# Row means on one core: two early stores divided by partitions into five DMAs

## The chip, the core and the metric

The kernel runs on one core of a Trainium2 chip. A core has engines that run side by side, each with its own instruction queue: VectorE (DVE in the profile), ScalarE (ACT), GpSimd (POOL), SyncE (SP) and TensorE (PE, unused here). Data move between the device's main memory and the core's on-chip memory of 128 partitions by DMA. An engine's queue issues a DMA, and 16 DMA engines carry out its packets in the background. When its part is through, each DMA engine adds to a semaphore, a counter on which an instruction of any engine can wait. The metric is device time in microseconds (us); lower is better. Before the change it is 160.59 us, the median of three runs (160.5 to 160.63).

## What is computed

The reference divides the sum of each row by a constant, 1024:

```python
batch, seq, dim = 32, 512, 1024
"x": np.random.randn(batch, seq, dim).astype(np.float32)
return (np.sum(x, axis=-1) / divisor).astype(np.float32)
```

That is 16,384 rows of 1,024 floats in (67.1 MB) and 16,384 floats out (0.07 MB).

## The kernel before

**Tiling.** The 16,384 rows are 128 per partition. They stand in two regions. In the first region partition p holds the 15 rows from 15p on; in the second it holds 113 rows, of which the first 97 are the "main" part and the last 16 the "last" part. So there are three outputs: `o_first` (15 floats per partition, 60 bytes), `o_main` (97 floats, 388 bytes, at a step of 113 floats) and `o_last` (16 floats, 64 bytes, in the gaps that `o_main` leaves). The results are gathered on chip in `res0`, `res` and `fin`; the profile calls both of the first two `res`.

**Loads and sums.** Every load is issued by SP through `load` (L182), in program order. They bring 2 and 13 rows per partition (first), then 14, 14, 14, 14, 14, 14 and 13 (main), then 9, 4 and 2 rows (last), and at the end one row in two halves, `pa` and `pb`. The large tiles rotate over three buffers, so a load waits until DVE is done with the tile that had its buffer. DVE reduces the rows of a tile with one instruction (L205); of the last two main tiles ACT takes 4 and 5 rows (L186). POOL multiplies a finished part by 1/1024 (L207). In the last part DVE sums single rows with the scale applied (L192), and ACT shares them. The row that comes in halves is summed last: first `pa` into a spare column of `pb`, then `pb` with that column into `fin`.

**Stores.** SP issues `o_first` (L223) and `o_main` (L224) after the load of `pb`, and `o_last` (L228) at the very end. One queue holds all of SP's DMAs; `tc.keep_in_program_order` fixes their order.

**Semaphores.** The framework gives the DMAs eight semaphores in turn. The seventeen DMAs are fourteen loads and three stores, so `o_first` has the seventh semaphore, `o_main` the eighth and `o_last` the first. Before a DMA is issued, SP waits until the DMA that used its semaphore before has landed, and a store also waits for the instruction that made its data.

**The end, written out by hand.** Three passes run over the finished program. `start_loads_at_once` (L19) moves the loads that wait for nothing ahead of the start barrier. `latest_wait_first` (L50) sorts an instruction's waits. `close_while_storing` (L69) moves the issue of `o_last` into the end sequence: SP first drains its other waits, joins the end barrier, then issues `o_last` when the semaphore `landed` says that DVE's last sum is there. Meanwhile POOL waits for all other DMAs and engines, clears the semaphores and releases the engines. SP's last instruction waits for `o_last` alone:

```python
last = nc.sync.wait_ge(landed, 17).ins
```

POOL's waits come from one list, which stands in the order POOL, ACT, DVE and then the DMA semaphores one to eight, and is compiled into five instructions with two waits each, in the order fourth and third, fifth and second, sixth and first, seventh and DVE, eighth and ACT, and one more for POOL itself.

Of the kernel before, what the change touches and what calls it, by code (L numbers as in the profile page):

```python
# [125 lines left out]
@with_exitstack  # L126
def kernel(
    ctx: ExitStack,
    tc: tile.TileContext,
    x: bass.AP,  # L130
    divisor: float,
    out: bass.AP,
):
    nc = tc.nc
    landed = nc.alloc_semaphore("landed")
    nc.at_finalize(start_loads_at_once)
    nc.at_finalize(latest_wait_first)
    nc.at_finalize(lambda nc: close_while_storing(nc, landed))
    xf = x.flatten_outer_dims()
    N, D = xf.shape  # L140
    P = nc.NUM_PARTITIONS
    scale = 1.0 / float(divisor)
    J = N // P
    assert J * P == N


    F, L = 15, 16
    M = J - F - L
    W = M + L
    x_first = bass.AP(tensor=x.tensor, offset=0, ap=[[F * D, P], [D, F], [1, D]])  # L150
    x_main = bass.AP(tensor=x.tensor, offset=P * F * D, ap=[[W * D, P], [D, M], [1, D]])
    x_last = bass.AP(tensor=x.tensor, offset=P * F * D + M * D, ap=[[W * D, P], [D, L], [1, D]])
    o_first = bass.AP(tensor=out.tensor, offset=0, ap=[[F, P], [1, F]])
    o_main = bass.AP(tensor=out.tensor, offset=P * F, ap=[[W, P], [1, M]])
    o_last = bass.AP(tensor=out.tensor, offset=P * F + M, ap=[[W, P], [1, L]])


    first = [(2, 0), (13, 0)]
    main = [(14, 0)] * 5 + [(14, 4), (13, 5)]
    last = [(9, 4), (4, 2), (2, 1)]  # L160
    assert sum(n for n, _ in first) == F
    assert sum(n for n, _ in main) == M and sum(n for n, _ in last) == L - 1

    pad = ctx.enter_context(tc.tile_pool(name="pad", bufs=1))
    pad.tile([P, 224], F32, name="pad")
    bulk = ctx.enter_context(tc.tile_pool(name="bulk", bufs=3))
    one = ctx.enter_context(tc.tile_pool(name="one", bufs=1))
    psum = ctx.enter_context(tc.tile_pool(name="junk", bufs=4, space=bass.MemoryType.PSUM))


    c = 512
    t4 = one.tile([P, 4, D], F32, name="t4")
    t2 = one.tile([P, 2, D], F32, name="t2")
    pa = one.tile([P, 768], F32, name="pa")[:, :c]
    pb = one.tile([P, D - c + 16], F32, name="pb")[:, : D - c + 2]
    res0 = one.tile([P, F], F32, name="res0")
    res = one.tile([P, M], F32, name="res")
    fin = one.tile([P, L], F32, name="fin")
    nc.gpsimd.memset(pb[:, D - c :], 0.0)  # L179

    def load(dst, src):
        tc.keep_in_program_order(nc.sync.dma_start(out=dst, in_=src))  # L182

    def act_sum(dst, src, by=1.0):
        junk = psum.tile([P, D], F32, name="junk")
        nc.scalar.activation(junk, src, COPY, scale=by, accum_out=dst)  # L186

    def dve_mean(dst, src, by=scale):


        h = src.shape[-1] // 2
        nc.vector.tensor_tensor_reduce(  # L192
            out=src[:, :h], in0=src[:, :h], in1=src[:, h:], scale=by, scalar=0.0,
            op0=ADD, op1=ADD, accum_out=dst,
        )

    for loads, src, dst in ((first, x_first, res0), (main, x_main, res)):
        j = 0
        for rows, on_act in loads:
            t = bulk.tile([P, 14, D], F32, name="t")  # L200
            load(t[:, :rows, :], src[:, j : j + rows, :])
            d = rows - on_act
            for i in range(d, rows):
                act_sum(dst[:, j + i : j + i + 1], t[:, i, :])
            nc.vector.reduce_sum(out=dst[:, j : j + d], in_=t[:, :d, :], axis=AX)  # L205
            j += rows
        nc.gpsimd.tensor_scalar_mul(out=dst, in0=dst, scalar1=scale)  # L207
    j = 0
    for rows, on_act in last:
        t = bulk.tile([P, 14, D], F32, name="t")[:, :rows, :] if rows > 4 else t4 if rows == 4 else t2  # L210
        load(t, x_last[:, j : j + rows, :])
        d = rows - on_act
        for i in range(rows):
            if i < d:
                dve_mean(fin[:, j + i : j + i + 1], t[:, i, :])
            else:
                act_sum(fin[:, j + i : j + i + 1], t[:, i, :], by=scale)
        j += rows
    load(pa, x_last[:, j, :c])
    load(pb[:, : D - c], x_last[:, j, c:])  # L220


    tc.keep_in_program_order(nc.sync.dma_start(out=o_first, in_=res0))  # L223
    tc.keep_in_program_order(nc.sync.dma_start(out=o_main, in_=res))  # L224

    dve_mean(pb[:, D - c : D - c + 1], pa, by=1.0)
    dve_mean(fin[:, j:], pb)
    tc.keep_in_program_order(nc.sync.dma_start(out=o_last, in_=fin))  # L228
# [35 lines left out]
```

## Time and profile before

| | |
|---|---|
| median of 3 runs | 160.59 us |
| span of the profiled execution | 159.1 us |
| profiled execution, to the last record of the runtime's semaphore | 160.53 us |
| DVE busy | 117.2 us (74% of the span) |
| ACT busy | 18.5 us (12%) |
| POOL busy | 1.0 us (1%) |
| DMA queue, share of 16 engines | 98.2% |
| memory traffic over the span | 422 GB/s |

The span runs from the first to the last instruction of the profiled execution; the times of the runs also hold what the runtime does around it, so they are some 1.5 us longer. An engine's busy time is the sum over its instructions; issuing DMAs and waiting for semaphores don't count as busy. A DMA's time to landing runs from the start of its issue to the last of its completion records and includes the time that it stands in the queue. Besides the views that are shown, the trace holds the start of every DMA packet with its size, and the time of every addition to a semaphore; where the text speaks of packet records, completion records or instruction records, it means these.

### The profile page before, as it was taken

How to read it: one execution, taken by the hardware profiler on the slowest of the kernel's cores; microseconds unless marked ns; L12 is line 12 of the kernel's file. 1: busy time of each engine (PE TensorE's matmuls, PEld its weight loads, DVE VectorE, ACT ScalarE, POOL GpSimd, SP SyncE). 2: the span in 40 equal slices, each digit the busy share in tenths (PEclk: the TensorE clock that was granted, in tenths of full speed). 3: DMA queues.
4: the chain of work that ended last, by engine and by line, in shares of the span. 5: the costliest groups of instructions: out<-in, count | busy, mean ns of one | idle time of the engine just before them, and what ended most of it. 6: DMA issues, size and time to landing. Idle time of an engine off the chain costs nothing.

```text
span 159.1 us, 148 instructions
## 1 busy us (share of the span) xinstructions
DVE 117.2 (74%) x29; ACT 18.5 (12%) x33; POOL 1.0 (1%) x7
## 2 busy tenths in 40 slices
DVE  0500089966999599959996899969995993398643
ACT  3000000000000000000000000000003700390684
POOL 0000000000000000000000000000000000001000
DMA  8999979999999789999998799999998999899894
GB/s 329 431 455 455 467 332 433 461 461 461 461 461 447 317 389 461 461 461 461 461 461 346 346 461 461 461 461 461 461 418 351 442 469 442 350 445 445 383 404 153
DMA packets 2448, 67.18 MB, mean 422 GB/s; under 512 B 656, under 2 KB 656, under 8 KB 912
## 3 DMA queue, kind: packets, MB, share of 16 engines
q1 hardware_dynamic: 2448, 67.18, 98.2%
HBM read 67.11 MB, written 0.07 MB: 422 GB/s over the span
## 4 chain that ended last, share of the span: by engine, by line
DMA 77%; DVE 21%; SPq 1%; issue 0%; DVEq 0%
DMA t<-in_x_dram 55%; DMA pb<-in_x_dram 22%; DVE res L205 20%; SPq L182 1%; DVE pb L192 0%; DVEq L259 0%
## 5 line engine op out<-in xcount | busy, mean ns | idle before, releaser
L205 DVE TENSOR_REDUCE res<-t 128x14 f32<-128x14336 f32 (+4 forms) x9 | 111.2, 12360 | 35.1 <-DMA t<-in_x_dram 35.1
L186 ACT ACTIVATE junk<-t 128x1024 f32<-128x1024 f32 x16 | 16.2, 1013 | 136.9 <-DMA t<-in_x_dram 136.9
L192 DVE CUSTOM_DVE_ANT_0 t<-t 128x512 f32<-128x512 f32 x8 | 5.1, 688 | 5.1 <-DMA t<-in_x_dram 5.1
L186 ACT ACTIVATION_READ_ACCUMULATOR junk<-t 128x1 f32 x16 | 3.0, 186 | 0.0
L207 POOL TENSOR_SCALAR res<-res 128x15 f32<-128x15 f32 (+1 forms) x2 | 0.7, 365 | 144.4 <-DVE res L205 144.4
L186 ACT ACT_TABLE_LOAD x1 | 1.3, 1283 | 1.7 <-PEq L245 1.7
L192 DVE DVE_READ_ACCUMULATOR2_ANT fin<- 128x1 f32 x9 | 0.7, 82 | 0.0
L192 DVE CUSTOM_DVE_ANT_0 pb<-pb 128x257 f32<-128x257 f32 x1 | 0.4, 429 | 0.2 <-DMA pb<-in_x_dram 0.2
L192 DVE CUSTOM_DVE_ANT_0 pa<-pa 128x256 f32<-128x256 f32 x1 | 0.4, 426 | 0.0
L179 POOL MEMSET pb<- 128x2 f32 x1 | 0.1, 100 | 1.3 <-POOLq L245 1.3
L245 POOL MEMSET const-bfloat16-1.0<- 128x1 bf16 x1 | 0.1, 102 | 0.0
L245 POOL MEMSET const-uint8-127<- 128x1 uint8 x1 | 0.1, 102 | 0.0
L245 POOL MEMSET const-float32-0.0<- 128x1 f32 x1 | 0.1, 100 | 0.2 <-issue 0.2
L245 POOL MEMSET const-float32-1.0<- 128x1 f32 x1 | 0.1, 99 | 0.0
L192 DVE DVE_READ_ACCUMULATOR2_ANT pb<- 128x1 f32 x1 | 0.1, 84 | 0.0
## 6 DMA issues: line engine op xcount, KB each, us to landing
t<-in_x_dram SPq DMA_DIRECT2D x6, 7168.0 KB, 36.0
t<-in_x_dram SPq DMA_DIRECT2D x2, 6656.0 KB, 27.2
t<-in_x_dram SPq DMA_DIRECT2D x1, 4608.0 KB, 28.4
t<-in_x_dram SPq DMA_DIRECT2D x2, 1024.0 KB, 19.8
t<-in_x_dram SPq DMA_DIRECT2D x1, 2048.0 KB, 32.9
pa<-in_x_dram SPq DMA_DIRECT2D x1, 256.0 KB, 35.1
pb<-in_x_dram SPq DMA_DIRECT2D x1, 256.0 KB, 35.2
out_dram<-res SPq DMA_DIRECT2D x1, 48.5 KB, 10.8
```

The source lines that it names most:

```text
L179: nc.gpsimd.memset(pb[:, D - c :], 0.0)
L182: tc.keep_in_program_order(nc.sync.dma_start(out=dst, in_=src))
L186: nc.scalar.activation(junk, src, COPY, scale=by, accum_out=dst)
L192: nc.vector.tensor_tensor_reduce(out=src[:, :h], in0=src[:, :h], in1=src[:, h:], scale=by, scalar=0.0, op0=ADD, op1=ADD, accum_out=dst,)
L205: nc.vector.reduce_sum(out=dst[:, j : j + d], in_=t[:, :d, :], axis=AX)
L207: nc.gpsimd.tensor_scalar_mul(out=dst, in0=dst, scalar1=scale)
L245: nc = _bacc.Bacc("TRN2", target_bir_lowering=False, num_devices=1)
```

## The change

The two early stores are cut by partitions. `o_first` becomes two DMAs, of partitions 0 to 119 and 120 to 127. `o_main` becomes three, of partitions 0 to 3, 4 to 115 and 116 to 127. All five are issued by SP after the load of `pb`, in this order, and each waits as a store did before: for POOL's scaled result and for the DMA that used its semaphore before. What is stored, and from and to where, stays. The program then has twenty DMAs in place of seventeen; `o_last` takes the fourth semaphore.

```diff
-    tc.keep_in_program_order(nc.sync.dma_start(out=o_first, in_=res0))
-    tc.keep_in_program_order(nc.sync.dma_start(out=o_main, in_=res))
+    def store(dst, src, *cuts):
+        for p0, p1 in zip((0, *cuts), (*cuts, P)):
+            tc.keep_in_program_order(nc.sync.dma_start(out=dst[p0:p1, :], in_=src[p0:p1, :]))
+
+    store(o_first, res0, 120)
+    store(o_main, res, 4, 116)
```

## The prediction

> **What bounds the kernel now.** I read the chain that ended last first, because it says which wait sets the end.
>
> ```profile
> DMA 77%; DVE 21%; SPq 1%; issue 0%; DVEq 0%
> DMA t<-in_x_dram 55%; DMA pb<-in_x_dram 22%; DVE res L205 20%; SPq L182 1%; DVE pb L192 0%; DVEq L259 0%
> ```
>
> No store is on it. In order of time its tail is the last load, one vector operation, and the end sequence:
>
> ```profile
> 121.91 35.22 DMA pb<-in_x_dram
> 157.12 0.02 issue
> 157.15 0.43 DVE pb L192
> 157.57 0.01 DVEq L259
> ```
>
> Next the DMA issues, columns KB and us from issue to landing, and then the SP queue's instructions in time:
>
> ```profile
> pb<-in_x_dram SPq DMA_DIRECT2D x1, 256.0 KB, 35.2
> out_dram<-res SPq DMA_DIRECT2D x1, 48.5 KB, 10.8
> out_dram<-res SPq DMA_DIRECT2D x1, 7.5 KB, 34.9
> out_dram<-fin SPq DMA_DIRECT2D x1, 8.0 KB, 1.4
> ```
> ```profile
> 122.39 0.48 SPq L223 DMA_DIRECT2D out_dram<-res  x1
> 146.95 0.34 SPq L224 DMA_DIRECT2D out_dram<-res  x1
> 157.61 0.33 SPq L228 DMA_DIRECT2D out_dram<-fin  x1
> ```
>
> The early stores are issued long before the end, but they queue behind pb: the first lands at 122.39 + 34.9 = 157.3, the second at 146.95 + 10.8 = 157.8, both after pb at 157.12. The last store goes out at 157.61 and lands at about 159.0. So the end is pb, then 0.45 of DVE, then 1.4 of the last store. What the DMA engines do there, by windows (the last two columns are DMA share and GB/s):
>
> ```profile
> 156.00:157.00 1.00, 0.98 (x4) 1.00 (x2) 0.00 (x0) 1.00 0.84 266
> 157.00:158.00 1.00, 0.43 (x2) 0.05 (x1) 0.00 (x0) 1.00 0.00 1
> 158.00:159.10 1.10, 0.00 (x0) 0.00 (x0) 0.00 (x0) 1.00 0.08 8
> ```
>
> The engines are empty for nearly all of 157 to 158; in the trace's packet records the early stores' last packet is at 157.05 and the last store's first at 158.44. Last, what SP waits for, and the end sequence by its lines:
>
> ```profile
> SPq L224 <- POOL res L207: 24.0, 1, 24.0
> SPq L259 <- ACT junk L186: 9.7, 1, 9.7
> SPq L105 <- SPq L105: 0.5, 1, 0.5
> ```
> ```profile
> L259 POOLq EVENT_SEMAPHORE  x9: 17/42/43, 155.9 to 158.5; - x9
> L105 SPq EVENT_SEMAPHORE  x1: 17/17/17, 159.0 to 159.0; - x1
> ```
>
> SP has 24.0 and 9.7 us of idle time around the second store. The 0.5 before L105 is the slack that matters: POOL, which collects every other completion, is through and has released SP by 158.57, and SP then waits for the last store until 159.05.
>
> **The sum's base.** The page gives the profiled execution a span of 159.1 (159.06 in the trace) and no total. Its records of the runtime's semaphore go on to 160.53, so that is its own time as far as the trace shows it, 0.06 under the median of 160.59. I carry differences to the median.
>
> **The change, part by part.** (1) Three more DMA issues on SP. The two kinds of row are 0.48 and 0.34, so 1.0 to 1.4 us of issue. One is added at about 122.9 inside the 24.0 wait, two at about 147.3 inside the 9.7 wait. Cost 0; if that cover were gone it would be the 1.4. Behind them on SP stands only the last store.
>
> (2) New waits on SP. The eight DMA semaphores are used in turn, and an issue first waits for the earlier DMA on its semaphore. Counting on from the loads: the 8-row piece waits for the sixth 14-row load (landed by 121.93), the 4-row piece for the 13-row load of the main part (137.69), the 112-row piece for the 9-row load (148.54), the 12-row piece for the 4-row load (153.40), the last store for the 2-row load (155.90); the times are the starts of the instructions that waited for these loads in the timeline. So the 112-row piece is issued at about 148.6, the 12-row piece at 153.4 to 153.8, not at 147. Both are still in the queue before pb's packets are through (156.3 to 156.8, 0.44 us between the first and the last engine). The last store's new wait is over 1.7 us before 157.61. Cost 0. The nearest row for how late an issue may be is the last store itself, 0.83 from issue to first packet: 153.8 + 0.8 = 154.6, 1.7 us of cover.
>
> (3) Packets. The bytes and the 256 row packets stay; completion packets grow with the pieces. In the packet records a 60 B packet takes 7 ns of its engine, a 388 B packet 20, a completion 9. If each piece spreads evenly, an engine that gets every remainder has one 60 B, one 388 B and three completions more: 7 + 20 + 27 = 54 ns; an engine left out of the remainders has less than before. All of it is behind pb and ahead of 158.44: 157.05 + 0.05 = 157.10. Cost 0, cover 1.3 us. The other end: one piece falls on a single engine, 112 x 20 ns = 2.24 us, and that engine is busy until about 159.0. I take even spreading, as each of the 17 DMAs here has 16 completion records, one per engine.
>
> (4) Landing of the early stores. The last packet to landing is 0.73 for the second store on its slowest four engines (157.05 to 157.78; the other twelve are in by 157.47), 0.39 for the last store, 0.30 for pb. The last piece therefore lands between 156.97 + 0.30 = 157.3 and 157.10 + 0.73 = 157.8; doubling the worst row gives 158.5. I take 157.7, by the row of the same kind.
>
> (5) POOL's end sequence. Before, POOL's instruction records show five two-semaphore waits: the 2-row and 4-row loads at 155.91, pa at 156.55, pb at 157.15, the first store at 157.32, the second at 157.80, the one that came last, and 0.77 later SP is released. The order goes by semaphore, not by time. After, the 12-row piece sits on the 4-row load's semaphore, thus in the first of the five, and the other four follow only then. The nearest row is 0.09 from that last wait to the instruction behind it, so 4 x 0.09 = 0.35 more. Release then at 157.7 + 0.02 + 0.77 + 0.35 = 158.84, against the last store's 159.05: still 0.2 earlier. Cost 0 to 0.1, I take 0.
>
> Sum: 0 on every part; pb, DVE and the last store untouched. 160.59 + 0.0 = 160.6.
>
> **A rule against it.** The row is the last store's 1.4 us from issue to landing, with SP idle around the early ones. The Trainium skill (DMA: Bandwidth & Descriptors, Rules for kernel authors) says transfers over separate parts of the partitions only serialize and should be one transfer, and its section on the anatomy of one DMA (for the GpSimd path) gives a fixed cost of about 2.0 us each; three more, if each were paid in turn, would be 6 us, 166.6 by an estimate from that page. The trace already shows pa and pb, each 35 us from issue to landing, overlapping.
>
> **The rivals.** (a) Slower by the collection on POOL. For it: step 5's wait order, with only 0.48 us of slack, and other engines that pass the runtime's end may need their release earlier still than SP. Against: the slack is larger than 0.35. It decides when the last piece lands after 157.90; over 0.2% needs 158.2. At 158.5 POOL releases at 159.64 rather than 159.05, 0.6 later: 161.2. At the limit where the slack outside SP's wait is nearer 0.2 than 0.48 and the landing stays 157.78, 0.15 later: 160.75.
>
> (b) Slower by a piece on too few engines. The 112-row piece on one engine ends at about 159.0 or after; that engine's part of the last store then starts at 159.0 in place of 158.5, 0.5 to 0.7 later: 161.1 to 161.3. It decides from about 80 rows on one engine. Against: no DMA here ran on fewer than 16, though none here has a row count other than 128.
>
> (c) Faster, because the last load or the last store no longer shares the slow engines with the early stores. For it: pb's engines end 0.44 apart, and if the stores of the early ones held back the late ones, up to 0.44 would come back, 160.15; the last store's landing of 0.39 could come down to pb's 0.30, 160.5. Against: the first load of the kernel, with no store in the queue, has the same spread (4.25 to 4.70). What lies behind the span, 1.5 us, is not explained by any row and could move either way.
>
> **How the numbers follow.** A measurement of this kernel can tell about 0.2%, 0.32 us, from no change. The main case, everything covered: 0.58, all within, its own range 160.35 to 160.85. Rival (a): 0.16, of it 0.14 slower and 0.02 within. Rival (b): 0.07, slower. Rival (c), with the unexplained end: 0.19, of it 0.17 faster and 0.02 within. So faster 0.17, same 0.62, slower 0.21. The range reaches to 160.15 for most of (c) and to 161.1 for most of (a) and the near end of (b).
>
> **What would show it.** Right: pb still lands at about 157.1 and the last store goes out some 0.5 later and takes 1.4; five early stores with issues near 122.4, 122.9, 147, 148.6 and 153.4, SP idle behind each; SP's last wait at L105 still over 0.1. Step 2 is wrong if the 112- and 12-row issues follow the 4-row one at once; step 3, if DMA share in 157 to 158 is no longer about 0; step 4, if a piece lands after 157.9; step 5, if POOL's five waits end together rather than one after the other. The forecast fails if SP's wait at L105 goes to 0 and the span grows (a), if the last store takes 1.9 or more (b), or if pb's landing moves (c).

## The result and the profile after

The changed kernel takes 161.05 us (median of 4 runs, 160.76 to 161.21) against 160.60 for the kernel before (4 runs beside it). The ratio is 1.0029, with a 95% interval of 1.0017 to 1.0042: 0.29% slower, 0.45 us. The profiled execution of the changed kernel is the slowest of its four, 161.21, with a span of 159.46. The kernel before has a span of 159.06, and its records put its profiled execution at about 160.42 (the last runtime record, less the 0.12 by which this record lies past the run's time in the other profiles). So the two profiled executions differ by 0.8, more than the medians do. The changed kernel was timed twice more in the experiments, at 161.24 and 161.26 against 160.53 and 160.64 for before beside it, 0.71 and 0.62 us slower.

The path that the chain shows has hardly moved. The tail of the chain in order of time, changed kernel (start, us, what):

```profile
122.05 35.12 DMA pb<-in_x_dram
157.16 0.02 issue
157.19 0.43 DVE pb L192
157.62 0.01 DVEq L263
```

pb lands at 157.16 in place of 157.12, and DVE's last sum is as long as before. The stores, in the view of SP's instructions and of the DMA issues (KB, then us to landing; for three of the pieces the view gives no landing):

```profile
122.53 31.20 SPq L225 DMA_DIRECT2D out_dram<-res  x5
157.65 0.36 SPq L232 DMA_DIRECT2D out_dram<-fin  x1
```
```profile
out_dram<-res SPq DMA_DIRECT2D x1, 42.4 KB, 9.5
out_dram<-res SPq DMA_DIRECT2D x1, 7.0 KB, 35.2
out_dram<-res SPq DMA_DIRECT2D x1, 0.5 KB
out_dram<-res SPq DMA_DIRECT2D x1, 1.5 KB
out_dram<-res SPq DMA_DIRECT2D x1, 4.5 KB
out_dram<-fin SPq DMA_DIRECT2D x1, 8.0 KB, 1.4
```

The five early stores are issued between 122.53 and 153.73, the last store goes out at 157.65 (before: 157.61) and still takes 1.4. The DMA engines stay empty after pb, by the window from 157 to 158 (the last two columns are DMA share and GB/s):

```profile
157.00:158.00 1.00, 0.44 (x3) 0.10 (x1) 0.00 (x0) 1.00 0.01 1
```

What moved is the end sequence. Its instructions by line (durations in ns, least, median and greatest; then the first and the last start) and SP's last wait:

```profile
L263 POOLq EVENT_SEMAPHORE  x9: 17/43/2347, 155.9 to 159.3; - x9
L263 SPq EVENT_SEMAPHORE  x3: 17/17/17, 155.9 to 159.4; - x3
L105 SPq EVENT_SEMAPHORE  x1: 17/17/17, 159.4 to 159.4; - x1
```

The last of SP's three is the one that POOL releases. The kernel before had it here:

```profile
L259 SPq EVENT_SEMAPHORE  x3: 17/17/17, 147.3 to 158.6; - x3
```

Before, POOL's nine semaphore instructions took at most 43 ns each and the last began at 158.5. Now one of them is held for 2.35 us and the last begins at 159.3, 0.8 later. SP's last wait begins at 159.4 although the last store has landed at 159.09, and the 0.5 of waiting before L105 is gone from the list of SP's waits. POOL's collection now ends after every other wait.

The instruction and completion records say how. The first of POOL's five two-semaphore waits holds the 12-row piece, whose last completion comes at 158.27. The four waits behind it follow at 0.087 each, and SP is released at 159.36. In the kernel before the last early completion is at 157.78 and the release at 158.57. The 0.80 between the releases is 0.49 of later landing and 0.31 of waits that stand behind the late one (four waits are 0.35; the step right after the late landing is 0.04 shorter than before).

### The profile page after: what moved, and what is told of

It reads as the page before. It is cut to its first block, busy times and chain, and to the rows that moved or that the text cites. A ratio compares the mean times of both kernels' runs of the same rounds, so it can differ in the third digit from the quotient of the medians.

```text
span 159.5 us, 151 instructions
## 1 busy us (share of the span) xinstructions
DVE 117.2 (73%) x29; ACT 18.5 (12%) x33; POOL 1.0 (1%) x7
## 4 chain that ended last, share of the span: by engine, by line
DMA 77%; DVE 21%; SPq 1%; issue 0%; DVEq 0%
DMA t<-in_x_dram 55%; DMA pb<-in_x_dram 22%; DVE res L205 20%; SPq L182 1%; DVE pb L192 0%; DVEq L263 0%
```

## The experiments

**The theory (A in the expectations).** POOL's release sets the time. It comes late for two reasons: more completions on a DMA engine land later, and the last piece's semaphore is first in POOL's order of waits. The rivals: the order costs nothing; pieces on fewer than 16 engines delay the landing by their shape rather than their number; or the added DMAs cost time in the queue itself, whoever waits for them.

**1. The order of POOL's waits turned (e1, and the same kernel again as e11, beside the changed kernel, e12).** The change stays, but the waits for the three pieces of `o_main` and the 8-row piece stand in the last two of the five instructions. The list of waits is put in a new order (`DMAHW0` is the first semaphore; `...` marks what is left out):

```diff
+ORDER = ('Pool_', 'DMAHW1_', 'DMAHW7_', 'DVE_', 'DMAHW5_', 'DMAHW3_', 'DMAHW4_', 'Activation_', 'DMAHW6_', 'DMAHW0_', 'DMAHW2_')
...
-            with_sync(i, on_wait=tuple(needs.values())) if i.name == gather.name else i
+            with_sync(i, on_wait=in_order(needs)) if i.name == gather.name else i
```

In the trace POOL's instructions then wait for fourth and fifth, ACT and sixth, seventh and DVE, first and eighth, second and third.

> The five pieces as changed; only the order of POOL's five end waits is other: the three o_main pieces and the 8-row piece stand in the last two. Theory A (two terms: the last piece lands 0.5 later because each further completion on a DMA engine takes about 0.2, and POOL's wait order adds 0.35 behind it): landing stays near 158.27, release 0.35 earlier, at about 159.05, level with the last store's landing; span 159.1 to 159.2, time 160.6 to 160.8. Theory B (the landing alone decides, the order costs nothing): no change, 161.05. Theory C (the loss is outside POOL's sequence): no change, and SP's last wait stays at 0.1.

Measured: 161.06 (5 runs; ratio to before 1.0034, 1.0022 to 1.0047), no better than the first timing of the changed kernel, but that one was made in another session with other runs of before. In the profile the release did come earlier, at 159.11, as theory A said, with the last landing at 158.32. So I ran it again with the changed kernel on one chip.

> The changed kernel with POOL's waits in the other order (the same kernel as e1), beside the changed kernel on one chip. Order worth 0.3: 0.25 to 0.35 below the changed kernel, 160.85 to 161.0. Order worth nothing, as e1 beside the first timing of the changed kernel looked: level.

> The changed kernel as it is, for the comparison with the reordered waits on this chip: 161.0 to 161.3.

Measured: 160.94 (11 runs; ratio 1.0017, 1.0008 to 1.0026) for the turned order against 161.26 (6 runs; ratio 1.0037, 1.0025 to 1.0049) for the changed kernel, a difference of 0.32. That is what POOL's records say of the order: from the last early landing to the release it is 1.10 us in the changed kernel and 0.79 in e1, 0.31 less. The first pair did not show it, and kernels timed apart can't be compared to better than some 0.2: against the before beside it, the turned order was slower by 0.50 in e1 and 0.30 in e11, the changed kernel by 0.45, 0.71 and 0.62. The second profile of the turned order (e11) shows one more thing: there pb itself landed late on a single DMA engine, at 157.76, and the last store with it.

**2. The order alone, in the kernel before (e4).** Nothing is cut; only the two early stores' semaphores are put into the first of POOL's waits.

```diff
+ORDER = ('Pool_', 'Activation_', 'DVE_', 'DMAHW0_', 'DMAHW1_', 'DMAHW6_', 'DMAHW7_', 'DMAHW4_', 'DMAHW5_', 'DMAHW2_', 'DMAHW3_')
```

POOL then waits for eighth and seventh, fifth and second, sixth and first, third and DVE, fourth and ACT.

> The kernel before, with only the order of POOL's end waits changed: the two early stores' semaphores are waited for first, four waits follow. It measures the order by itself. Theory A: landing 157.78 as before, release 0.35 later at 158.92, still ahead of the last store at 159.05: span 159.1, time 160.6 if SP's slack is the only one, up to 160.8 if the other engines need their release earlier than SP.

Measured: 161.05 (5 runs, 160.81 to 161.47; ratio 1.0033, 1.002 to 1.0045). It is 0.49 slower than before, about as much as the change in its first timing, with no store cut. In the profiled execution (161.47, the slowest) the end sequence reads:

```profile
L266 POOLq EVENT_SEMAPHORE  x9: 17/43/43, 158.5 to 159.6; - x9
L266 SPq EVENT_SEMAPHORE  x3: 17/17/17, 147.5 to 159.6; - x3
```

POOL's first wait is met only at 158.5, because ten completions of the second store came at 158.19 to 158.48 that time. So two things moved the release in this execution, 0.70 of later landing and 0.35 of order, and the order's own share is better read from e11 and e12. The execution still refutes the prediction's slack. The release came 1.05 later than in the kernel before (159.62 for 158.57), and the time rose by 1.05 as well (161.47 for about 160.42), while the end of SP's last instruction moved by only 0.65. Had the time gone by SP's end, as the prediction had it, it would have risen by 0.65.

**3. Each cut alone (e2, then e3).**

```diff
-    store(o_main, res, 4, 116)
+    store(o_main, res)
```

> Only o_first is cut (120 and 8); o_main whole. Theory A: three completions on up to eight engines in place of two, landing 157.78 + 0.2 = 157.98; o_main's semaphore is in POOL's third wait, two waits follow, + 0.17; release 158.95, still under 159.05: span 159.1, time 160.6 to 160.7. If pieces on fewer than 16 engines by themselves delay the landing (theory B2), the landing is near 158.27 and the span 159.3.

Measured: 160.91 (11 runs; ratio 1.0021, 1.0012 to 1.0031), more than expected. The landing is 158.14 and two waits stand behind it (0.14).

```diff
-    store(o_first, res0, 120)
+    store(o_first, res0)
```

> Only o_main is cut (4, 112, 12); o_first whole. Theory A: four completions on the engines with every remainder, landing 157.78 + 2 x 0.2 = 158.1 to 158.2; the 12-row piece is in POOL's second wait, three follow, + 0.26; release 159.15 to 159.25, 0.1 to 0.2 over the last store: span 159.2 to 159.3, time 160.75 to 160.95. If the cut of o_first carries the loss, 160.6.

Measured: 160.81 (11 runs; ratio 1.0018, 1.001 to 1.0027), as expected in time, with a landing of 157.94, earlier than expected, and 0.22 of waits behind it. Neither cut carries the loss alone. They are 0.35 and 0.25 over before; the sum, 0.60, is level with the change itself (0.45, 0.71 and 0.62 in its three timings). The two landings don't go by the count of completions: the DMA engines that had most had three with the first cut (158.14) and four with the second (157.94). With one profile of each, a count can't be told from the spread here; the next two experiments can.

**4. Five even pieces (e5, beside the changed kernel, e8).** As many DMAs as in the change, but each of a multiple of 16 partitions, so that each has 16 completions.

```diff
-    store(o_first, res0, 120)
-    store(o_main, res, 4, 116)
+    store(o_first, res0, 112)
+    store(o_main, res, 16, 112)
```

> Five early stores again, but cut so that each has a multiple of 16 partitions (112 and 16; 16, 96 and 16), so every piece has 16 completions, one per engine. Revised theory A (POOL's second release sets the end: time = last early landing + what POOL's remaining waits cost + 2.64, the sum that the runs so far share to 0.01): what counts is the number of completions on an engine, and that is five on all of them: landing 158.2 to 158.5, time 161.05 to 161.4. Theory B (pieces on 8, 4 or 12 engines delay the landing by their shape): landing back at 157.8 to 158.0, time 160.75 to 160.95.

> The changed kernel as it is, on the same chip as the other three, for their comparison and for the spread of its landing: 160.8 to 161.2, last early landing 158.0 to 158.4.

Measured beside each other: 161.25 (5 runs; ratio 1.0046, 1.0033 to 1.0058) and 161.24 for the changed kernel itself (5 runs; ratio 1.004, 1.0027 to 1.0054). The shape is not it. The landings of the even pieces show the cost plainly. The last completion of pb and of each store after it, in the order of the queue:

```
pb 157.35   stores 157.53  157.71  157.87  158.05  158.25
```

The steps are 0.17 to 0.20. Each further completion behind the last load took this long, though its packet is recorded at 9 ns, and of a piece of 16 partitions an engine has one data packet of at most 24 ns. The fourth piece has 96 partitions, six data packets to an engine, and its step is no longer than the others. The records don't name the engine of a completion; that the steps are those of one engine is read from all 16 records moving alike.

**5. Six even stores (e10).**

```diff
-    store(o_first, res0, 120)
-    store(o_main, res, 4, 116)
+    store(o_first, res0)
+    store(o_main, res, 16, 32, 48, 112)
```

> o_first whole, o_main in five pieces of 16, 16, 16, 64 and 16 partitions: six completions on every engine. If each completion behind the last load takes its engine about 0.18 (the step between the early stores' first and last landings in the even-cut kernel), the last piece lands 6 x 0.18 = 1.1 after pb at 157.2 to 157.3, at 158.3 to 158.5, and with POOL's four waits behind it the time is 161.3 to 161.5, some 0.1 to 0.2 over the five even pieces. If a random delay of single engines decides and not the count, no more than the five: 160.9 to 161.25.

Measured: 161.55 (5 runs; ratio 1.0054, 1.0042 to 1.0066), 0.3 over the five pieces, which ran on another chip (0.2 when each is taken against the before beside it), and 0.3 over the changed kernel on the same chip (161.26). The completion records, first and last of each store:

```
       pb      stores
first  156.79  156.97  157.14  157.32  157.49  157.66  157.84
last   157.28  157.69  157.89  158.10  158.29  158.49  158.70
```

The first completions step by 0.17 and the last by 0.20. The last ones also carry a delay of 0.41 rather than 0.2 at the first store. So the count sets the steps, and on top of them some engines are late by some tenths, in one execution more than in another.

**6. SP waits for the early stores instead of POOL (e6 and e7, then e9).** The stores' completions go to a semaphore that POOL doesn't collect, and SP waits for it at its very end, beside the last store's. First the changed kernel, then the kernel before.

```diff
+    stored = nc.sync.wait_ge(early, 80).ins      # 32 in the kernel before
...
+        else with_sync(i, on_update=on_early("sem-add-imm", 16)) if i.name in firsts
...
+        with_sync(stored, on_update=on_early("sem-sub-imm", 80)),
         with_sync(last, on_update=update("sem-sub-imm", 17)),
```

> The changed kernel, but the five stores' completions go to a semaphore of their own for which SP waits at its very end, beside the last store's; POOL no longer waits for any store. Revised theory A: POOL's waits end with pb and with DVE's part of the barrier at 157.65, its second release comes at 158.3 rather than 159.36, and the whole loss goes: 160.1 to 160.5, at or below the kernel before; how far below says where SP's wait for the last store begins to bind. Rival (the loss lies in the queue or in DGE work of the added DMAs, not in POOL's wait for them): it stays near 161.0.

> The kernel before, with the same move of its two early stores' completions from POOL to SP. Revised theory A: POOL's wait for the second store set the end here too, so it gains: 160.1 to 160.5, the same as the changed kernel with that move. Rival (before was bound by SP's wait for the last store, as the prediction read L105): 160.56, no change.

Measured: 160.78 (11 runs; ratio 1.0013, 1.0004 to 1.0022) and 160.51 (11 runs; ratio 0.9997, 0.9988 to 1.0006). The first is above the 160.1 to 160.5 that theory A expected. The changed kernel ran at 161.24 on that chip, so most of the loss goes with POOL's wait. The kernel before gains nothing from the same move, against theory A too: it was not bound by POOL alone. What is left of the loss, 0.25, came with a late pb (157.49 in the profile). So I gave each of the five stores a semaphore of its own:

> As e6 (the changed kernel, SP instead of POOL waits for the five early stores), but each store has a semaphore of its own. e6 was left 0.25 above before, with pb's last two engines 0.3 behind the others. If the 80 additions to one semaphore caused that: 160.5, level with e7. If the five DMAs behind pb cost it themselves (through pb's landing and the longer issue of the last store, 0.36 for 0.33): 160.75 again.

Measured: 160.70 (11 runs) against 160.64 for the kernel before beside it, ratio 1.0001 (0.9992 to 1.001). With five cut stores in the queue the time of the kernel before is back. The end sequence of this profile, POOL's instructions and SP's, and what SP waits for last:

```profile
L276 POOLq EVENT_SEMAPHORE  x9: 17/43/43, 156.0 to 158.4; - x9
L276 SPq EVENT_SEMAPHORE  x3: 17/17/17, 156.0 to 158.4; - x3
L114 SPq EVENT_SEMAPHORE  x1: 17/17/17, 159.2 to 159.2; - x1
```
```profile
SPq L114 <- SPq L114: 0.4, 1, 0.4
```

POOL is through at 158.4 (changed kernel: 159.3), and SP again waits 0.4 for the last store, although the last piece lands at 158.23, as late as in the changed kernel. This shows the cause by removal: the same DMAs, the same landing, and no loss that the timing can tell once POOL doesn't wait for it. Whether the 0.25 that the shared semaphore kept is the sharing or the spread of pb's landing (the two were timed on different chips) stays open.

**What the profiles say together.** Two sums bound every profiled execution: SP's second release by POOL (the last of SP's three semaphore instructions in the end sequence) plus 1.85, and the end of SP's last instruction plus 1.32. The larger one is the time. The two constants are fitted to these same executions, 1.85 where the release decides and 1.32 in the four rows where SP's end does; two numbers then give all 13 known times to 0.01 (the repeats e8 and e12 of the changed kernel, not in the table, too):

| kernel | last early landing | release + 1.85 | SP's end + 1.32 | profiled run |
|---|---|---|---|---|
| before | 157.78 | 160.42 | 160.38 | not given |
| changed | 158.27 | 161.21 | 160.78 | 161.21 |
| waits turned (first) | 158.32 | 160.96 | 160.52 | 160.96 |
| waits turned (again) | 158.29 | 160.93 | 161.03 | 161.04 |
| order alone | 158.48 | 161.47 | 161.03 | 161.47 |
| first store cut | 158.14 | 160.92 | 160.50 | 160.91 |
| second store cut | 157.94 | 160.80 | 160.56 | 160.80 |
| five even | 158.25 | 161.20 | 160.76 | 161.20 |
| six even | 158.70 | 161.68 | 161.24 | 161.69 |
| changed, SP waits | 158.19 | 160.52 | 160.78 | 160.78 |
| before, SP waits | 157.86 | 160.30 | 160.56 | 160.56 |
| changed, SP waits, own semaphores | 158.23 | 160.27 | 160.53 | 160.53 |

The two constants differ by 0.53: what follows POOL's release lasts that much longer than what follows SP's own last wait. The trace shows where the two meet. Behind the kernel's end the runtime's semaphore has 18 records. The first four come 0.30, 0.33, 0.54 and 0.58 after the release in all 14 profiles. The fifth follows SP's end by 0.13 to 0.14, but comes no earlier than 0.60 after the release; the sixth is some 0.04 behind the fifth, but no earlier than 0.70 after the release:

| kernel | SP's end after the release | fifth record after the release | sixth | last |
|---|---|---|---|---|
| before | 0.50 | 0.64 | 0.70 | 1.97 |
| changed | 0.10 | 0.60 | 0.70 | 1.97 |
| waits turned (again) | 0.64 | 0.78 | 0.82 | 2.09 |
| changed, SP waits, own semaphores | 0.79 | 0.92 | 0.97 | 2.23 |

So SP's own end delays what follows only when it comes more than about 0.53 after the release. In the kernel before it came 0.50 after it. The 0.48 by which SP's wait outlasted the release was therefore no slack of the release: the release already set the time in that execution, and SP's wait had 0.04 to spare.

## Why the prediction was right or wrong

The time, 161.05, lies in the range, but 0.05 from its upper end and outside the main case's own 160.35 to 160.85. That it lies inside is in part luck: the repeats, 161.24 and 161.26, lie outside. The mechanism of the main case, everything covered, was wrong. The case that came true is rival (a), the collection on POOL, which had a chance of 0.16, and the prediction's own signs say so: a piece landed after 157.9, and SP's wait at L105 went to nothing while the span grew from 159.06 to 159.46. The base, 160.53 for the profiled execution, was some 0.12 too high, which a sum of zeros does not feel. The 166.6 of the rule against it did not come either: the three further DMAs cost 0.45 to 0.71 together.

**Steps 1 and 2 held.** SP's idle time hid the three issues and the new waits. The 112-row piece was issued at 148.58 and the 12-row piece at 153.43, where step 2 had put them, and pb and the last store came as before.

**Step 3 held for the packets and failed for what they stand for.** The last early packet ends at 157.08, as computed (157.10). But the step priced a completion at the 9 ns of its packet. Behind the last load one completion follows another by 0.17 to 0.20. The kernel before has a hint of it, had I read it so: the first completions of pb and of the first store are at 156.68 and 156.86, 0.18 apart, with only eight packets of 7 ns and a completion's between them. (The next, at 157.03, tells nothing: eight packets of 20 ns fill its 0.17.) Three more on an engine are 0.5 to 0.6. The Trainium skill (DMA: Bandwidth & Descriptors, Anatomy of one DMA, which is about the GpSimd path) says that a DMA's semaphore update waits until its last byte is confirmed in the target memory. A wait of that kind, taken in turn, would look like these steps, but these DMAs are SP's, and no run here shows what the steps are made of.

**Step 4 is the term that was mis-sized.** It put the last landing at 157.7; it was 158.27 (158.21 and 158.25 in the repeats). The 0.49 against before is about what three added completions come to, but one profile doesn't prove it, for late single engines move the landing by as much: with no store cut it was 157.78, 157.86 (e7) and 158.48 (e4). That the count matters is shown by the steps of the even pieces.

**Step 5 had the order right and its size (0.35 for 0.31), and compared it with the wrong slack.** It took the time between SP's release and SP's last wait for free. Rival (a) named the doubt, that other engines may need their release earlier than SP, but priced it with 0.2 of slack left and decided by a landing after 157.90. There was none: in the profile of the kernel before the release set the time already, so a later release counts in full.

**Rival (b)** fell: the pieces of 120, 8, 4, 112 and 12 partitions had 15, 8, 4, 16 and 12 completions after pb, so each spread over many engines, and the profile's packet count rose by 23, from 2448 to 2471. In the Trainium skill (DMA: Bandwidth & Descriptors, Why a DMA increments its semaphore by 16 and not by 1) the number of engines is the largest up to 16 that divides the partition counts; the trace agrees in all five. **Rival (c)** fell too: neither pb nor the last store came earlier.

## What to carry to other kernels

Where an engine collects completions before it lets the others go, ask what still runs after its release: a wait that ends later elsewhere gives slack only if the same amount of work follows it. Small stores behind the last load are priced by their completions, read from how far apart they land, and not by their packets. When a semaphore changes hands, look at where it stands in a list of waits: if it is met last and stands early, every other wait comes behind it (0.087 us each here).

## What was not expected of the hardware

A completion of a small store behind the last load follows the one before by 0.17 to 0.20 us, though its packet takes 9 ns. Stores that are cut unevenly get the additions of the engines that they don't use at once: the 4-row piece's semaphore had its first record at 147.42, right after its issue, and the rest at 157.36 to 157.52. Landings near the end spread between executions: the kernel with the order changed alone lands its second store at 158.48, 0.7 after the kernel before with the same DMAs, and one engine's pb came 0.6 after the other fifteen in one profile. What makes single engines late is open.
